# One pass over the tokens, weights packed for single reads, x transposed by layout, and pooling by doubling sums on VectorE, in a hybrid decoder layer on eight cores

## The chip, the cores and the metric

The kernel runs on all 8 cores of one Trainium2 chip. Each core works on its own half of one of four sequences (2048 tokens), so no core waits for another core's data. The metric is the device time of the slowest core, in microseconds (us).

Some executions show a slower state: the cores of one die, or of both, have a lower granted TensorE clock in the records, and the run is some per cent longer. Cores 0 to 3 are die 0, cores 4 to 7 are die 1.

## The reference, cut to what matters

This is an outline and not the code itself.

```python
D_MODEL = 2048; BATCH = 4; SEQ = 4096            # 3 branches of width 1024 each
POOL_WINDOWS = (2, 4, 8, 16)

h = rmsnorm(x, norm_pre)
xa, ga, u, vb, gb, q, gc = split_cols(h @ w_in)  # w_in: 2048 x 7168
ya = pool_mixer(xa, w_pool, scale) * silu(ga)    # A: trailing means minus token, then 256x256 map per group
yb = spatial_gating(u, vb, ...) * silu(gb)       # B: 128x128 causal mixing within chunks of 128 tokens
yc = memory_cross_attention(q, k_m, v_m) * silu(gc)   # C: 4 heads, 256 memory tokens
y = concat([rmsnorm(ya, g_a), rmsnorm(yb, g_b), rmsnorm(yc, g_c)])
out = x + rmsnorm(y @ w_out, norm_post)          # w_out: 3072 x 2048
```

The pool mixer averages, for each of four channel groups, the last 2, 4, 8 or 16 tokens, subtracts the token itself, and applies a 256 x 256 map. Each branch needs a sum of squares over its 1024 channels for every token; both kernels compute it with matmuls against a column of ones, one result column for each tile of 128 tokens.

## The kernel before

The kernel goes over its 2048 tokens in two passes of 1024, and reads the input and output weights once in each pass. It loads x with tokens on the partitions, normalises it, and transposes it on TensorE. In each pass the order is: v and spatial gating (B), pooling (A), attention (C), projection out.

```python
D = 2048; TC = 2048; TP = 1024; NPASS = TC // TP
...
def w_view(src_d, c0):       # 256 columns of the weight: runs of 1 KB in memory
    return src_d[:, c0:c0 + 256].rearrange("(k p) c -> p k c", p=128)
...
def finish_y(p, br, chunk_in_br, tb, pre_fn, pre_reads):
    flush_ss(keep=1)         # the sum of squares of an earlier chunk; the last one stays back
    ...
    P.op("dve", lambda e: pre_fn(e, tmp), ...)
    P.op("act", ... yT3[:, c, ...] = tmp * gain ...)
    P.op("act", ... sq = Square(tmp) ...)
    def ss_group():
        ...                  # 4 matmuls, lhsT=sq (128 tokens each), rhs=ones column
    guard["pending_ss"].append(ss_group)
...
for p in range(NPASS):
    ...
    norm_transpose_many(items, norm_pre_d, after_b=after_b)   # x in, 16 transposes a tile on TensorE
    ...
    xcp_tok = dma_sp(out_d[p * TP:(p + 1) * TP, :], x_d[p * TP:(p + 1) * TP, :], sem="d_xcp")
    for g in range(4):       # pooling: band matrices on TensorE
        ...
        fns += [mm(o, xa_tm[:, tt + 1, cols], mcur[:, g, :], True, False),
                mm(o, xa_tm[:, tt, cols], mprev[:, g, :], False, True)]
```

The copy of x into the output (the residual is added to it at the end by an accumulating DMA) is issued once a pass, at the start of pooling. And a chunk's sum-of-squares matmuls are held back (`keep=1`) until the chunk after it has been emitted, so that TensorE has other work while ScalarE squares.

## Time and profile before

| | before |
|---|---|
| time, median of 3 runs | 1513.77 us (1500.56 to 1519.29) |
| TensorE busy, profiled core | 1281 of 1513 us |
| first steady TensorE work | at 106 us |
| dense stretch: 712 matmuls of 512 columns | 153.7 us, 215.9 ns each |
| read from memory, profiled core | 231 MB |

The first lines are from the page of the kernel before: busy time and share of the span by engine; then the span in 40 slices, in tenths, for TensorE, for its granted clock and for the DMA engines; then the DMA queue of the weights (packets, MB, share of the engines' time) and the memory traffic.

```profile
PE 1281.3 (85%) x7936; PEld 732.4 (48%) x7936; DVE 437.6 (29%) x704; ACT 513.9 (34%) x936; POOL 109.0 (7%) x109
...
PE   0267869999996999999970579899999999999991
...
PEclk9988979999998999999995789999999999999996
DMA  9974999885669954454599959995955364414549
...
q0 software_dynamic: 160400, 109.58, 60.0%
...
HBM read 230.93 MB, written 33.55 MB: 175 GB/s over the span
```

TensorE is the limit: it is busy 85% of the time, and most slices read 9. What is lost lies at the start, in the middle where the second pass begins, and at the end. The windows view of the same kernel gives the busy time of five engines in each stretch (with instruction counts), then the granted clock, the DMA share and GB/s:

```profile
106.00:218.00 112.00, 84.32 (x632) 60.84 (x632) 46.70 (x78) 48.59 (x72) 6.85 (x6) 0.87 0.78 135
240.00:400.00 160.00, 160.00 (x1125) 98.42 (x1123) 34.66 (x56) 42.09 (x78) 12.55 (x11) 1.00 0.74 76
...
782.00:857.00 75.00, 18.38 (x117) 12.71 (x116) 18.64 (x21) 11.48 (x19) 6.66 (x7) 0.60 1.06 194
857.00:968.00 111.00, 90.80 (x697) 66.32 (x695) 49.53 (x84) 54.56 (x82) 6.86 (x6) 0.91 0.87 151
```

The dense stretch (240 to 400 us) has nothing to give: TensorE is busy for all of it at clock 1.00. The change of pass (782 to 857 us) has 18 us of matmuls in 75 us with the DMA engines full. The TensorE timeline of that place (start, duration, work, and in brackets the idle time before it with its releaser) shows what it waited for:

```profile
825.51 1.86 PE L312 MATMUL ps<-ident,yT 128*128 128x128 bf16 x16 [39.34 <-DVE stat L279]
...
835.04 7.09 PE L309 MATMUL ps<-wpool,hT 128*128 128x256 bf16 x48 [5.14 <-DMA out<-stg]
853.60 3.57 PE L309 MATMUL ps<-wpool,hT 128*128 128x256 bf16 x16 [11.47 <-DMA wpool<-w_in]
```

Normalisation, the stores of the first pass and the weights are all late there, one after the other.

### The profile page before, as it was taken

How to read it: one execution, taken by the hardware profiler on the slowest of the kernel's cores; microseconds unless marked ns; L12 is line 12 of the kernel's file. 1: busy time of each engine (PE TensorE's matmuls, PEld its weight loads, DVE VectorE, ACT ScalarE, POOL GpSimd, SP SyncE). 2: the span in 40 equal slices, each digit the busy share in tenths (PEclk: the TensorE clock that was granted, in tenths of full speed). 3: DMA queues.
4: the chain of work that ended last, by engine and by line, in shares of the span. 5: the costliest groups of instructions: out<-in, count | busy, mean ns of one | idle time of the engine just before them, and what ended most of it. 6: DMA issues, size and time to landing. Idle time of an engine off the chain costs nothing.

```text
span 1513.0 us, 20596 instructions; the slowest of 8 cores (1488.0 to 1513.0 us)
## 1 busy us (share of the span) xinstructions
PE 1281.3 (85%) x7936; PEld 732.4 (48%) x7936; DVE 437.6 (29%) x704; ACT 513.9 (34%) x936; POOL 109.0 (7%) x109
## 2 busy tenths in 40 slices
PE   0267869999996999999970579899999999999991
PEld 0156624467774445444430466445776444444440
DVE  0335412311110222322271244222111222232253
ACT  0345412223230465422221354222322466532220
POOL 2000100000011000000011001001000000000000
PEclk9988979999998999999995789999999999999996
DMA  9974999885669954454599959995955364414549
GB/s 150 202 182 120 164 112 102 87 85 57 68 71 154 130 80 56 56 78 67 65 155 204 203 134 167 114 110 56 107 62 65 48 81 67 77 15 70 84 77 146
DMA packets 171135, 156.23 MB, mean 103 GB/s; under 512 B 6560, under 2 KB 165024, under 8 KB 165792
## 3 DMA queue, kind: packets, MB, share of 16 engines
q0 software_dynamic: 160400, 109.58, 60.0%
q1 hardware_dynamic: 10640, 45.34, 13.2%
q8 instruction: 65, 1.06, 0.3%
q14 instruction: 30, 0.25, 0.1%
HBM read 230.93 MB, written 33.55 MB: 175 GB/s over the span
## 4 chain that ended last, share of the span: by engine, by line
PE 74%; DMA 14%; DVE 3%; issue 2%; ACT 2%; SPq 2%; another core or an unknown queue 1%; POOL 0%; DVEq 0%; ACTq 0%; POOLq 0%
PE ps L309 73%; DMA wpool<-w_in 7%; DMA out<-stg 3%; DMA yT<-mem_norm 1%; DMA yT<-norm_pre 1%; SPq L358 1%; DMA yT<-sgu_ln_g 1%; PE ps L312 1%; ACT stg L651 1%; DVE stg L887 1%; SPq L321 1%; ACT junk L633 1%; ACT junk L630 1%; DVE yT L368 0%
## 5 line engine op out<-in xcount | busy, mean ns | idle before, releaser
L309 PE MATMUL ps<-hT,wpool 128*128 128x512 bf16 x2560 | 572.5, 382 | 21.9 <-DMA wpool<-w_in 21.9
L309 PEld LDWEIGHTS ps<-hT,wpool 128*128 128x128 bf16 x2560 | 248.6, 98 | 311.2 <-issue 31.6
L309 PE MATMUL ps<-wpool,yT 128*128 128x512 bf16 (+1 forms) x1600 | 339.8, 375 | 0.0
L309 PE MATMUL ps<-wpool,hT 128*128 128x256 bf16 x2048 | 246.0, 285 | 39.2 <-ACT stg L651 21.7
L309 PEld LDWEIGHTS ps<-wpool,yT 128*128 128x128 bf16 x1600 | 155.9, 98 | 180.9
L309 PEld LDWEIGHTS ps<-wpool,hT 128*128 128x128 bf16 x2048 | 208.2, 102 | 72.9 <-issue 40.9
L522 ACT ACTIVATE yT<-stg,gbr 128x512 bf16<-128x512 f32 x96 | 68.8, 716 | 222.1 <-DVE stg L697 150.7
L312 PE MATMUL ps<-ident,yT 128*128 128x128 bf16 x304 | 27.7, 264 | 123.3 <-DVE stat L279 101.2
L324 POOL DMA_DIRECT2D wpool<-w_in x56 | 64.2, 1158 | 808.8 <-PE ps L309 426.4
L550 ACT ACTIVATE stg<-ps 128x512 f32<-128x512 f32 x96 | 55.5, 596 | 113.7 <-PE ps L309 113.4
L312 PEld LDWEIGHTS ps<-ident,yT 128*128 128x128 bf16 x304 | 24.6, 120 | 126.3 <-issue 126.0
L915 DVE SCALAR_TENSOR_TENSOR hT<-ps,stat,hT 128x512 f32<-128x512 f32 x64 | 48.1, 751 | 91.3 <-PE ps L309 80.7
L683 DVE TENSOR_TENSOR stg<-ps,stg 128x512 f32<-128x512 f32 x32 | 22.1, 692 | 174.5 <-PE ps L309 170.1
L564 DVE CAST stg<-ps 128x512 bf16<-128x512 f32 x32 | 22.1, 692 | 131.8 <-PE ps L309 130.9
L526 ACT ACTIVATE stg<-stg 128x512 bf16<-128x512 f32 x96 | 58.8, 613 | 0.0
L918 ACT ACTIVATE junk<-hT 128x512 bf16<-128x512 f32 x32 | 20.2, 630 | 106.9 <-DVE hT L915 84.2
L763 DVE SCALAR_TENSOR_TENSOR stg<-ps,pscale,stg 128x512 f32<-128x512 f32 x32 | 22.6, 747 | 106.0 <-PE ps L532 106.0
L368 DVE SCALAR_TENSOR_TENSOR yT<-yT,stat 128x2048 bf16<-128x2048 f32 x19 | 44.7, 2352 | 28.8 <-DMA yT<-norm_pre 24.3
L365 ACT ACTIVATE yT<-yT 128x2048 bf16<-128x2048 f32 x19 | 36.1, 1902 | 39.5 <-DMA yT<-x 39.5
L324 POOL DMA_DIRECT2D wpool<-w_out x24 | 21.0, 874 | 345.5 <-PE ps L309 161.8
L564 DVE CAST vnr<-ps 128x256 bf16<-128x256 f32 x32 | 13.6, 425 | 100.4 <-PE ps L309 89.7
L279 DVE RECIPROCAL stat<-stat 128x1 f32<-128x1 f32 (+1 forms) x53 | 8.9, 167 | 112.9 <-ACT stat L277 112.9
(98 smaller groups left out, 886.1 us busy)
## 6 DMA issues: line engine op xcount, KB each, us to landing
wpool<-w_in POOLq DMA_DIRECT2D x56, 1024.0 KB, 23.0
wpool<-w_out POOLq DMA_DIRECT2D x24, 1024.0 KB, 11.5
yT<-x SPq DMA_DIRECT2D x16, 1024.0 KB, 11.3
wpool<-w_kv POOLq DMA_DIRECT2D x8, 1024.0 KB, 13.0
out<-hT POOLq DMA_DIRECT2D x8, 1024.0 KB, 15.3
out<-vnr POOLq DMA_DIRECT2D x4, 1024.0 KB, 22.2
out<-stg POOLq DMA_DIRECT2D x4, 1024.0 KB, 26.9
yT<-mem SPq DMA_DIRECT2D x2, 1024.0 KB, 23.4
```

Source lines behind the costliest of these rows:

```text
L309: return lambda e: e.matmul(out, lhsT=lhsT, rhs=rhs, start=start, stop=stop)
L312: return lambda e: e.transpose(out, in_, ident[:])
L324: return P.op("pool", lambda e: e.dma_start(out=out, in_=in_), reads, writes, dma_sem=sem)
L365: P.op("act", lambda e: e.activation(out=xs, in_=xt, func=AF.Square, accum_out=sc(col_ss)), reads=[xb], writes=[xsb, stb], waits=guard.get ...
L368: P.op("dve", lambda e: e.scalar_tensor_tensor(out=xs, in0=xt, scalar=sc(col_rs), in1=gb_v, op0=ALU.mult, op1=ALU.mult), reads=[xb, gbc, s ...
L522: P.op("act", lambda e: e.activation(out=yT3[:, c, tb * 512:(tb + 1) * 512], in_=tmp, func=AF.Copy, scale=gbr[:, c:c + 1]), reads=[tmp_b[i ...
L526: P.op("act", lambda e: e.activation(out=sq, in_=tmp, func=AF.Square), reads=[tmp_b[i]], writes=[sq_b[i]])
L550: P.op("act", lambda e: e.activation(out=stg_sil[i], in_=psb(b), func=AF.Silu), reads=[bank[b]], writes=[sil_b[i]])
L564: P.op("dve", lambda e: e.tensor_copy(out=out, in_=in_), reads=reads, writes=writes, waits=waits)
L683: P.op("dve", lambda e, si=si, bu=bu: e.tensor_tensor(out=stg_sil[si], in0=psb(bu), in1=stg_sil[si], op=ALU.mult), reads=[bank[bu], sil_b[ ...
L763: return e.scalar_tensor_tensor(out=tmp, in0=psb(by), scalar=pscale[:, ch:ch + 1], in1=stg_sil[si], op0=ALU.mult, op1=ALU.mult)
L915: P.op("dve", lambda e, b=bks[br], orow=orow, c=rc + br * 8 + tt: e.scalar_tensor_tensor(out=orow, in0=psb(b), scalar=sc(c), in1=orow, op0 ...
```

## The change

The intent is to remove everything that happens twice and everything that only moves data on TensorE: one pass over 2048 tokens, so each input weight is read once; weights repacked so that a partition reads 8 KB in a row; x handed over already transposed; the pooling means by doubling sums on VectorE (a window of 16 takes four shifted additions) in place of band matmuls; the output projection in two groups of 7 and 9 token tiles. Branch order becomes A, C, B. Cut to its core, with cuts marked:

```diff
-TP = 1024
-NPASS = TC // TP
...
-    def w_view(src_d, c0):
-        return src_d[:, c0:c0 + 256].rearrange("(k p) c -> p k c", p=128)
+    w_d = din("wst", [NCH, 128, 2048])            # packed
+    def load_group(key, waits=()):
+        ...
+            dma_pool(dst, w_d[c], writes=[M_ring(sl)], sem=f"d_w{sl}", waits=waits)
...
-        norm_transpose_many(items, norm_pre_d, after_b=after_b)
+    def norm_x(tb):                                # x transposed by layout
+        ... Square on ScalarE; 16 matmuls against a 128x128 block of ones
+        rstd_bc(b, 512)                            # Sqrt, then reciprocal of 128x512
+        ... 16 multiplies of 128x512 on VectorE
...
+    late = []
+    def flush(n=0):
+        while len(late) > n:
+            late.pop(0)()
+    def pair_ss(br, tb, first, last):
+        P.op("pool", lambda e: e.tensor_tensor(out=sqp[:], in0=sq[0][:], in1=sq[1][:], op=ALU.add), ...)
+        def f():
+            ... P.group("pe", fns, reads=[M_sqp, "ones"], writes=[bk(0)])   # 4 one-column matmuls
+        late.append(f)
...
-                            fns += [mm(o, xa_tm[:, tt + 1, cols], mcur[:, g, :], True, False),
-                                    mm(o, xa_tm[:, tt, cols], mprev[:, g, :], False, True)]
+    def a_block(g, tb, split=False):
+        for cc in range(2):
+            ... proj(r0 + cc, tb, b, split and cc == 0)
+            a_chain(g, cc, tb, b)                  # copy, 1 to 4 additions, combine (VectorE)
+            if cc == 0:
+                flush()
+        ... 2 more projections with silu
+        def pool_part():
+            ... 4 matmuls, scale on VectorE, finish_y (ScalarE), twice
+            pair_ss(0, tb, g == 0, g == 3)         # appends to late again
+        late.append(pool_part)
...
-        xcp_tok = dma_sp(out_d[p * TP:(p + 1) * TP, :], x_d[p * TP:(p + 1) * TP, :], sem="d_xcp")
+    for j in range(4):                             # emitted in the gating branch
+        ...
+        xcp.append(dma_sp(out_d[j * 512:(j + 1) * 512, :], x_d[j * 512:(j + 1) * 512, :], sem=f"d_xc{j}"))
...
+    for half in range(2):                          # projection out, 7 and then 9 tiles
```

## The prediction

> **What bounds the kernel now.** TensorE. The page's busy table gives PE 1281 of 1513 us; the chain that ended last is 73% matmul. Dense stretches cannot shrink: in the windows 240–400, 640–760 and 1320–1480 us PE is 100% busy at granted clock 1.00, and 712 matmuls of 512 columns take 153.7 us (215.9 ns each). The loss, by windows and chain: PE works steadily only from 106 us; the first v stage runs from 106 to 218 us for about 57 us of matmuls, the second (after an empty stretch, 782–857) to 968; weight waits end both (44 and 36 us) and another comes before the memory projection (31 us); 33 us of tail. Matmuls counted from the program at dense rates (216, 109 and 60 ns for 512, 256 and up to 128 columns) make about 1249 us, so about 264 us are idle or slow clock.
>
> **What changes.** One pass removes the boundary (about 130 us lost at 780–968), the second read of the input weights (184 MB to 126 MB of source), and the 1 KB runs of the weight DMAs. Transposed x removes 304+ transposes and their evictions, but adds 64 ones-matmuls and 16 VectorE multiplies of 512 per block. Pool matmuls leave PE for two to five VectorE operations per half-group. Matmul work falls only to about 1227 us.
>
> **New cost, from the built order on PE.** In the pooling branch each block's deferred part is emitted after the next block's first projection, and its own sum-of-squares matmuls immediately follow. These wait for: ScalarE copy (0.6), 1–4 adds of 512 (0.7 each and about 0.1 between, as dependent VectorE operations show), combine (0.75), two scale operations, copy and square twice (in the trace 3.2 us from the first scale to the last square), then a GpSimd add. The Trainium skill, GPSIMD Engine Reference, section 3.1, has 4497 ns for a 2048-element add; estimate 1.2 us for 512; no add on GpSimd is in this trace. PE covers 0.9 us of it, so stalls of 6.4–8.8 us, and near 19 us where a block's normalisation stands ahead on VectorE (twice; 13 for memory). Sixteen flushes: about 153 us. The Trainium skill, TensorE: Matmul & The Clock Gate, Part 1, says about 3.4 us idle drops the clock; the trace agrees (64 short matmuls take 9.3 us after a pause, 7.15 dense; clock 0.83–0.87 in the v stages). About 2 us per stall: 30 us.
>
> **Sum (estimate).** Steady PE start 54 us (4 MB of x, normalisation, 2 more MB at about 200 GB/s, the rate of busy slices) + 1227 + 153 + 30 + 20 (branch joins, first output weights, half change) + 31 tail = 1515 us. All of it is critical, as PE is: pooling stalls about return the gains.
>
> **What would show it.** First steady PE work 50–65 us; no gap near half time; in the pooling stage (to about 500 us) PE 60–65% busy with a regular 6–9 us gap per block before the one-column matmuls, released by POOL, clock under 0.95; attention, gating and output above 95% busy at 1.00; DMA share lower.
>
> **What would make it wrong.** A GpSimd add under 0.5 us or over 3; the clock not falling in stalls (−25 us); x arriving late (+20); dense matmuls throttled below 1.00 because PE is busier (+5% or more); output weights, read twice, falling behind 12 us per 2 MB.
>
> Predicted 1515 us, 1462–1568 eight times in ten; faster by over 2%: 0.28, within 2%: 0.48, slower: 0.24.

## The result and the profile after

| | before | after |
|---|---|---|
| time, median of fast runs | 1513.12 us (4 runs) | 1589.63 us (4 runs, 1587.03 to 1593.79) |
| ratio after / before | | 1.052, 95% interval 1.0448 to 1.0591 |
| read from memory | 231 MB | 165 MB |
| TensorE busy | 1281 us | 1298 us |
| first steady TensorE work | 106 us | 51 us |

Ratios here are the mean time of one kernel's fast runs over that of the other's fast runs of the same rounds, so they are not quite the ratio of the medians quoted. The changed kernel is correct, and slower. The prediction was wrong: it had said 1515 us, with 1568 at the top of its range, and had given "slower" 0.24.

The same lines of the page of the kernel after, with the two groups that matter (line, engine, operation, shapes, count, then busy time, mean ns, idle time before them and what ended it):

```profile
PE 1297.9 (82%) x6242; PEld 588.7 (37%) x6242; DVE 525.0 (33%) x868; ACT 434.5 (27%) x781; POOL 126.4 (8%) x165
...
PE   2755457777675896699998999999998999799990
...
PEclk9887779798887787799999999999998999899995
DMA  9910109333300599703303006033125559973279
...
q0 software_dynamic: 21136, 80.22, 33.1%
...
HBM read 164.93 MB, written 33.55 MB: 125 GB/s over the span
...
L510 PE MATMUL ps<-arena 128*128 128x1 bf16 x192 | 11.7, 165 | 158.9 <-POOL arena L503 158.9
...
L503 POOL TENSOR_TENSOR arena<-arena 128x512 bf16<-128x512 bf16 x48 | 55.1, 1148 | 891.9 <-ACT arena L499 878.4
```

The DMA engines are much freer, the gap in the middle is gone, and TensorE starts in half the time. But the first third of the span now reads 4 to 7 in the busy slices and 7 to 9 in the clock slices: that is the pooling branch, which runs to 537 us. The waits view (line waited at, what ended the wait, total us, times, longest) names three waits of TensorE:

```profile
PE ps L510 <- POOL arena L503: 158.9, 19, 19.3
PE ps L364 <- ACT arena L430: 43.7, 13, 15.6
PE ps L364 <- DMA arena<-wst: 42.9, 3, 28.2
```

The first is the one that matters. The second is mostly the start, while x arrives. One case of the first, from the timeline of all engines, with L531 a doubling addition, L537 the combination, L577 the scale by gate, L496 and L499 the scaled copy and the square on ScalarE, L503 the addition on GpSimd and L510 the one-column matmuls:

```profile
74.31 0.69 DVE L531 TENSOR_TENSOR arena<-arena 128x512 f32<-128x512 f32 x1 [0.83 <-ACT arena L525]
75.11 0.69 DVE L537 SCALAR_TENSOR_TENSOR arena<-arena 128x512 bf16<-128x512 f32 x1
...
76.02 1.41 DVE L577 SCALAR_TENSOR_TENSOR arena<-ps,arena 128x512 f32<-128x512 f32 x2
...
78.63 0.61 ACT L499 ACTIVATE arena<-arena 128x512 bf16<-128x512 f32 x1
79.39 1.14 POOL L503 TENSOR_TENSOR arena<-arena 128x512 bf16<-128x512 bf16 x1 [58.73 <-ACT arena L499]
...
80.68 0.24 PE L510 MATMUL ps<-arena 128*128 128x1 bf16 x4 [6.31 <-POOL arena L503]
```

This is one chain of dependent work, with TensorE standing idle for 6.31 us of it. The reason is in the source: `flush` runs the deferred `pool_part`, which appends the sum of squares to the same list, and the `while` loop runs that at once. Deferral works for the matmuls of the pooling map and not for the sum of squares behind them.

The second cost is the clock, and it shows best in windows of 2 us around one such stall, which here lasts from 274.3 to 281.18 us (columns as above; the third number from the end is the clock):

```profile
276.00:278.00 2.00, 0.00 (x0) 0.00 (x0) 1.81 (x3) 0.75 (x2) 0.00 (x0) 1.00 0.93 174
278.00:280.00 2.00, 0.00 (x0) 0.00 (x0) 0.00 (x0) 1.62 (x3) 0.11 (x1) 0.63 0.38 76
...
283.00:285.00 2.00, 2.00 (x6) 0.71 (x5) 0.00 (x0) 0.00 (x0) 0.00 (x0) 0.50 0.62 92
...
287.00:289.00 2.00, 2.00 (x11) 0.94 (x10) 1.15 (x2) 0.58 (x1) 0.53 (x1) 1.00 0.02 4
```

About 4 us into the pause the clock falls to 0.50. It stays there until about 4 us after work has resumed: TensorE does 6 matmuls in 2 us where it later does 11. "Busy" does not show this. The mean clock of the whole window 260 to 537 us is 0.83, but that is not a level at which TensorE ever runs for long: it is a mixture of 1.00 and 0.50, and of one more level that comes next. The Trainium skill, TensorE: Matmul & The Clock Gate, Part 1, has this gate: half clock after an idle window of about 3.4 us, full clock after as long a stretch of work. This trace agrees: over the 16 stalls of pooling on core 6, the clock fell 2.1 to 5.2 us after the pause began and came back 3.1 to 6.1 us after work had resumed.

The third cost comes in attention. These are the TensorE timeline there; then the issues of SyncE's queue; then the DMA views, by queue for 560 to 620 us, in which both queues had work (packets, MB and share of the engines' time), and by issue for 530 to 660 us (KB each and median us from issue to landing):

```profile
620.41 0.70 PE L701 MATMUL ps<-arena 128*128 128x128 bf16 x8
649.29 10.99 PE L364 MATMUL ps<-arena 128*128 128x512 bf16 x39 [28.18 <-DMA arena<-wst]
```

```profile
533.68 2.54 SPq L368 DMA_DIRECT2D out<-x  x4
```

```profile
q1 hardware_dynamic: 169, 8.52, 81.9%
q0 software_dynamic: 176, 0.66, 13.7%
...
arena<-wst POOLq DMA_DIRECT2D x8, 512.0 KB, 56.3
...
out<-x SPq DMA_DIRECT2D x4, 74.1
```

The four copies of x into the output (4 MB each) stand in the gating branch in the source, in a loop that runs from about 970 us. But nothing that they wait for ties them to it, so SyncE issues them as soon as it comes to them, at 533.68 us, the moment when attention loads its second group of weights. That group landed around 649 us, and TensorE waited 28 us for it. From 560 to 620 us the two queues sent nearly equal numbers of packets (169 and 176), but those of the copies' queue are larger, 50 KB against 4 KB on average (MB over packets), so it had 82% of the engines' time. The Trainium skill, DMA: Bandwidth & Descriptors, section on queues, rings and completion order, says that an engine alternates between its queues packet by packet; the two counts agree with it, if the profile's packets are those that the page means.

There is a fourth, smaller thing. On cores 2, 3, 6 and 7 the clock read 0.81 whenever it was not 0.50, from about 500 to 659 us, through dense work; on cores 0, 1, 4 and 5 attention ran at 1.00. Core 6 ended at 1589.1 us and core 0 at 1577.5.

### The profile page after: what moved, and what is told of

Its sections match the earlier page's. It is cut to its first block, busy times and chain, and to the rows that moved or that the text cites. A ratio compares the mean times of both kernels' runs of the same rounds, so it can differ in the third digit from the quotient of the medians.

```text
span 1589.1 us, 17429 instructions; the slowest of 8 cores (1577.5 to 1589.1 us)
## 1 busy us (share of the span) xinstructions
PE 1297.9 (82%) x6242; PEld 588.7 (37%) x6242; DVE 525.0 (33%) x868; ACT 434.5 (27%) x781; POOL 126.4 (8%) x165
## 4 chain that ended last, share of the span: by engine, by line
PE 76%; DVE 8%; ACT 4%; DMA 4%; issue 3%; another core or an unknown queue 2%; POOL 1%; DVEq 0%; ACTq 0%; POOLq 0%; SPq 0%
PE ps L364 75%; DVE arena L439 2%; DMA arena<-wst 2%; DVE arena L531 2%; DMA arena<-xT 2%; POOL arena L503 1%; ACT arena L499 1%; ACT arena L430 1%; DVE arena L577 1%; DVE arena L420 1%; ACT arena L496 1%; DVE arena L949 1%; DVE arena L537 1%; PE ps L510 1%
## 5 line engine op out<-in xcount | busy, mean ns | idle before, releaser
L364 PE MATMUL ps<-arena 128*128 128x512 bf16 (+3 forms) x5922 | 1289.6, 380 | 94.9 <-ACT arena L430 43.7
L364 PEld LDWEIGHTS ps<-arena 128*128 128x128 bf16 x5922 | 574.7, 101 | 785.2 <-issue 236.5
L496 ACT ACTIVATE arena<-arena 128x512 bf16<-128x512 f32 x96 | 68.8, 716 | 428.8 <-DVE arena L839 173.1
L931 DVE SCALAR_TENSOR_TENSOR arena<-ps,arena 128x512 f32<-128x512 f32 x128 | 95.9, 750 | 204.0 <-PE ps L364 184.9
L510 PE MATMUL ps<-arena 128*128 128x1 bf16 x192 | 11.7, 165 | 158.9 <-POOL arena L503 158.9
L531 DVE TENSOR_TENSOR arena<-arena 128x512 f32<-128x512 f32 (+5 forms) x80 | 55.7, 697 | 224.3 <-ACT arena L525 219.3
L503 POOL TENSOR_TENSOR arena<-arena 128x512 bf16<-128x512 bf16 x48 | 55.1, 1148 | 891.9 <-ACT arena L499 878.4
L935 ACT ACTIVATE ps<-arena 128x512 f32<-128x512 f32 x64 | 38.5, 601 | 227.5 <-DVE arena L931 191.9
L371 POOL DMA_DIRECT2D arena<-wst x96 | 56.5, 601 | 453.0 <-PE ps L364 434.6
L833 DVE SCALAR_TENSOR_TENSOR arena<-ps,arena 128x512 f32<-128x512 f32 x32 | 24.0, 751 | 154.8 <-PE ps L364 83.3
L510 PEld LDWEIGHTS ps<-arena 128*128 128x128 bf16 x192 | 9.6, 100 | 173.3 <-issue 172.8
L517 ACT ACTIVATE arena<-ps 128x512 f32<-128x512 f32 x64 | 37.1, 596 | 82.5 <-PE ps L364 81.9
L499 ACT ACTIVATE arena<-arena 128x512 bf16<-128x512 f32 x96 | 58.8, 613 | 0.0
L928 ACT ACTIVATE arena<-ps,arena 128x512 f32<-128x512 f32 x64 | 43.3, 683 | 24.6 <-PE ps L364 11.7
L439 DVE SCALAR_TENSOR_TENSOR arena<-arena 128x512 bf16<-128x512 f32 x64 | 42.8, 745 | 0.4
## 6 DMA issues: line engine op xcount, KB each, us to landing
arena<-wst POOLq DMA_DIRECT2D x72, 512.0 KB, 13.5
out<-arena POOLq DMA_DIRECT2D x16, 1024.0 KB, 14.9
```

The costliest lines, as they stand in the source:

```text
L364: return lambda e: e.matmul(out, lhsT=lhsT, rhs=rhs, start=start, stop=stop)
L371: return P.op("pool", lambda e: e.dma_start(out=out, in_=in_), reads, writes, waits, dma_sem=sem)
L439: P.op("dve", lambda e, i=i, k=k: e.scalar_tensor_tensor(out=hT[:, k, tb * 512:(tb + 1) * 512], in0=xp[i % 6][:, k % 4, :], scalar=cp[:, C ...
L496: P.op("act", lambda e: e.activation(out=yT[:, c, tb * 512:(tb + 1) * 512], in_=tmp[ti][:], func=AF.Copy, scale=cp[:, CP_GBR + c:CP_GBR + ...
L499: P.op("act", lambda e: e.activation(out=sq[si][:], in_=tmp[ti][:], func=AF.Square), reads=[M_tmp[ti]], writes=[M_sq[si]])
L503: P.op("pool", lambda e: e.tensor_tensor(out=sqp[:], in0=sq[0][:], in1=sq[1][:], op=ALU.add), reads=[M_sq[0], M_sq[1]], writes=[M_sqp])
```

## The experiments

The theory: the time went into (1) stalls of TensorE at the sum of squares, (2) a lower clock, and (3) the weights that arrive behind the copies. Rivals: that the lower clock does not belong to the stalls but to the first part of the kernel or to all cores working at once, and that the wait in attention is not due to the copies. Experiments e1, e2, e3 and e4 ran where the kernel before had many slow runs (its two fast ones took 1511.54 and 1512.35 us); e3 again, e5 and e6 where it took 1510.15 us (median of 11).

### e1: hold the sum of squares back by one more block

```diff
-    def flush(n=0):
-        while len(late) > n:
+    def flush():
+        for _ in range(len(late)):
             late.pop(0)()
...
     def branch_rstd():
-        flush()
+        while late:
+            flush()
```

> Edit: each flush emits only what was waiting when it began, so a pooling block's sum-of-squares matmuls come one block (about 15 us of TensorE work) later than the pool matmuls they depend on. Theory P (placement): the 159 us that PE waits for the GpSimd add in front of these matmuls fall below 30 us. Rival V (the VectorE work itself, norms and doubling sums, cannot keep up): the wait only moves to pool matmuls or to PSUM banks, and the time stays above 1540 us. On the clock, theory B (the stop-and-go of the pooling stage trips the lower clock): granted clock in the dense pooling stretches and in attention goes from about 0.81 to 1.00, time 1390 to 1440 us. Rival E (the clock is low in the first 600 us for another cause): clock stays 0.81 to about 620 us and the time is 1450 to 1490 us.

Correct; one fast run, 1423.77 us, and three slow ones. The waits view of core 0, which had an undisturbed die:

```profile
PE ps L364 <- DMA arena<-wst: 57.0, 3, 43.5
...
PE ps L510 <- POOL arena L503: 12.0, 4, 5.3
```

On core 0 the wait for GpSimd fell from 159.2 to 12.0 us. The span of that core fell from 1577.5 to 1416.9 us, by more than the wait, because the clock came back with it: adding up windows of 1 us (busy time times one minus the clock), the time that TensorE lost to a lower clock fell from 53 to 19 us. Part was given back: the wait for weights grew from 48.5 to 57.0, since attention now starts earlier and runs into the same copies.

### e2: tie the copies of x to the gating branch

```diff
             pair_ss(1, tb, j == 0, j == 3)
+            if tb == 0:
+                xcp.append(dma_sp(out_d[j * 512:(j + 1) * 512, :], x_d[j * 512:(j + 1) * 512, :],
+                                  sem=f"d_xc{j}", waits=[("e_pe", P.count["e_pe"])]))
...
-    xcp.append(dma_sp(out_d[...], x_d[...], sem=f"d_xc{j}"))
```

> Edit: the four copies of x into the output wait for TensorE to reach the gating stage, instead of all starting together where attention starts. Theory D (the 28 us wait for weights at 621 us is this collision): the wait goes, the copies land in the gating stage. On the clock: if the lower clock is released by time or by the end of the bursts, the gain is about 28 us (1561 us). If it was released by the 28 us pause itself, the attention stage goes on at 0.81 after 650 us and the gain is eaten: 1580 us or slower, in the worst case 1650.

Correct; the three fast runs took 1561.40, 1561.97 and 1583.40 us (two more were slow), ratio to before 1.04 (1.0087 to 1.0713), too wide an interval to call it slower by 2%. The wait of TensorE at GpSimd is unchanged, 158.9 us. The weights wait of the slowest core fell from 42.9 to 14.6 us, and its longest from 28.2 to 7.3:

```profile
PE ps L364 <- DMA arena<-wst: 14.6, 2, 7.3
```

So the copies were the cause. The gain in time, 28 us (medians of fast runs, 1561.97 against 1589.63), is smaller than what core 0 gained (1577.5 to 1536.9, 41 us). Windows of core 0 and of core 4, the slowest, show why:

```profile
537.00:600.00 63.00, 61.45 (x320) 29.49 (x326) 25.24 (x50) 30.44 (x60) 5.55 (x7) 1.00 0.19 35
```

```profile
540.00:657.00 117.00, 116.06 (x513) 51.84 (x512) 40.83 (x84) 47.33 (x92) 7.84 (x9) 0.81 0.23 35
657.00:720.00 63.00, 62.38 (x337) 29.83 (x335) 24.27 (x49) 29.72 (x59) 6.69 (x8) 0.99 0.21 34
```

Cores 4 and 5 held the clock 0.81 from about 497 to 659 us, through dense work, and then had full clock without any pause. In the kernel after, the cores with the lower clock were partly forgiven it: they arrived later at a wait that ended at a time set by the DMA (28.2 us on core 6, 35.4 on core 0). With that wait gone they pay in full.

### e3: both together

The edits of e1 and e2.

> Both edits. Theories P, B and D together: no wait over 8 us in pooling after the normalisations, clock near 1.00, 1360 to 1410 us, faster than both kernels. If the gains overlap (the pause hides other waits), no better than the deferral alone.

Correct; fast runs 1375.41 and 1395.96 us, ratio 0.9165 with a wide interval (0.8872 to 0.9457), four slow runs.

> The same kernel as in the earlier run of both edits, repeated for a ratio from more fast runs: most runs there were in the slow state. Expected: fast runs at 1370 to 1380 us, ratio to before 0.90 to 0.92.

Median 1375.55 us of five fast runs (a sixth was slow), ratio to before 0.9135 (0.9099 to 0.9171). This version beats both kernels. The windows of core 0 in this repeat, in pooling and in attention:

```profile
200.00:350.00 150.00, 149.20 (x831) 75.39 (x844) 71.05 (x112) 37.73 (x69) 17.75 (x24) 1.00 0.54 89
...
460.00:520.00 60.00, 59.44 (x312) 28.34 (x317) 25.12 (x55) 32.05 (x63) 6.69 (x8) 1.00 0.22 36
```

Pooling now has TensorE busy for 149 of 150 us at clock 1.00, with the additions on VectorE and GpSimd as before. So the place of the work was not the fault; the point where its result was asked for was. From the kernel after to e3, core 0 went from 1577.5 to 1366.9 us, by 211: the wait at GpSimd fell by 147 us (159.2 to 12.2), the weights wait by 36 (48.5 to 12.8), the time lost to the clock by 39 (53 to 14), and other waits grew by about 12. On the same core the first edit alone gave 161 us and the second alone 41, which is 202 of the 211; the other 9 us are about what the first alone had given back in the wait for weights.

### e4: move the flush in front of the additions of the block

A second way to shorten the stall, by a changed order on VectorE alone: the deferred scale operations go ahead of the new block's doubling additions.

```diff
             proj(r0 + cc, tb, b, split and cc == 0)
-            a_chain(g, cc, tb, b)
             if cc == 0:
                 flush()
+            a_chain(g, cc, tb, b)
```

> Edit: in the kernel after, the deferred part is emitted ahead of the next block's doubling sums instead of behind them, sum-of-squares placement unchanged. Theory P as costed: each stall is a sum of terms and loses the ScalarE copy, the sums and the combine, 2.4 to 4.8 us per block, while scale, copy, square, GpSimd add (about 5 us) stay: waits of 159 us fall to about 95 to 110 us, time 1525 to 1545 us. If the doubling sums were not part of the stall, no change.

One fast run, 1537.31 us. The wait at GpSimd fell from 158.9 to 110.5 us, still 19 times:

```profile
PE ps L510 <- POOL arena L503: 110.5, 19, 16.7
```

So 48 us of the stalls were the additions standing ahead on VectorE. Of the rest, three stalls (16.3, 16.7 and 13.5 us) still have a normalisation ahead of them on VectorE, and the others, 4.3 to 4.5 us in pooling, are the chain from the scale to GpSimd. The clock gave nothing back: 76 us of the pooling stage's work still ran at 0.50 on core 2, against 77 on core 6 of the kernel after, with as many stalls, though shorter ones. Time and wait moved together: 52 us of time for 48 of wait. That this run also had a spell of the clock 0.81 on cores 2 and 3 (433 to 576 us), as the kernel after had, leaves a few us of it open.

### e5: put the stall back, in attention

The test for the clock. To e3, one line: after each attention block the sum of squares is asked for at once.

```diff
         pair_ss(2, tb, hh == 0, hh == 3)
+        flush()
```

> Both edits kept, but now the attention stage (another stage, with other VectorE and DMA work) gets the placement that pooling had: its sum-of-squares matmuls right behind the matmuls they depend on. By the chain (two multiplies, copy and square twice, GpSimd add) each of the 16 blocks stalls 4 to 5 us, as the one such place between attention and gating did in the kernel after (4.5 us): 65 to 80 us in all. Theory B (stop-and-go work itself brings the lower clock): on an undisturbed die the granted clock of the attention stage falls from 1.00 to 0.80 to 0.88 and its dense stretches slow by 15 to 20%, a further 25 to 45 us; fast time 1470 to 1500 us. Rival E (the low clock belonged to the pooling stage or to the first 600 us): clock stays at or above 0.95 apart from the pauses, time 1440 to 1455 us.

1483.14 us (two fast runs), ratio to before 0.9835 (0.9788 to 0.9881), 108 us more than e3. All 8 cores lay between 1474.8 and 1480.8 us. Pooling kept its clock of 1.00. Attention on core 0, around one of the new stalls of 4.55 us (416.4 to 420.92 us):

```profile
412.00:417.00 5.00, 4.31 (x20) 1.76 (x18) 2.39 (x5) 0.01 (x1) 0.00 (x0) 1.00 0.00 0
...
423.00:425.00 2.00, 2.00 (x7) 0.62 (x5) 0.96 (x3) 1.59 (x2) 0.00 (x0) 0.50 0.00 0
...
427.00:434.00 7.00, 6.95 (x33) 3.19 (x33) 0.86 (x2) 2.50 (x4) 0.00 (x0) 1.00 0.00 0
```

The wait at GpSimd grew from 12.2 to 80.2 us on core 0, by 68:

```profile
PE ps L510 <- POOL arena L503: 80.2, 19, 5.3
```

From 360 to 820 us, where attention lies, TensorE did 87 us of its work at clock 0.50, against 5 in e3, which is 41 us more lost. The two make 109 of the 110 us by which this core's span grew. The rival that the low clock belongs to the first 600 us or to pooling falls: the same pooling runs at 1.00, and attention, which ran at 1.00 in e3, loses its clock when pauses of 4.5 us are put in. These pauses cost, beyond themselves, more than half as much again in clock (41 us beside 68).

### e6: interleave the blocks with the normalisation

With the stalls gone, the largest wait of e3 is for the squares of x at the start (ScalarE, 51.9 us on core 0). This run emits a pooling block between the normalisations, in the hope of filling it.

```diff
     norm_x(0)
     norm_halo()
-    norm_x(1)
     a_block(0, 0, True)
+    norm_x(1)
+    a_block(1, 0)
     a_block(0, 1, True)
     norm_x(2)
...
```

> Both edits, and the blocks of the first two pooling groups reordered so that a normalisation always has a whole block of matmuls in front of it (first block ahead of the second normalisation; the buffer of the pooled differences rotated so that neighbours do not share it). In the run of both edits TensorE still waited 52 us for the squares and about 12 us for VectorE in the first 200 us. If those waits are only order: 20 to 35 us less, fast runs 1340 to 1355 us. If x arrives too slowly (about 17 MB of x and weights by 100 us), less than 10 us.

A miss: 1389.08 us (median of three fast runs; a fourth was slow), ratio 0.9213 (0.9178 to 0.9248), 14 us slower than e3. The waits of core 0:

```profile
PE ps L364 <- ACT arena L430: 28.4, 14, 11.6
PE ps L364 <- DVE arena L454: 19.7, 1, 19.7
PE ps L510 <- POOL arena L503: 16.2, 5, 5.0
```

The wait aimed at fell by 23.5 us, but a new one of 19.7 took its place: the first block needs the normalised 16 tokens ahead of the half, and those now stand directly in front of it. The later normalisations now stand behind pooling work in the emitted order, and the wait for the memory's squares (L464) grew from 3.4 to 11.8 us. The wait moved, and did not go. What an order that wins here would look like is open.

## Why the prediction was wrong

Two terms of its sum failed: the lower clock (30 us predicted, 72 measured) and the other waits (20 predicted, 58 measured). The sum can be measured term by term. The terms for core 6, the slowest of the profiled run, and for core 0, which had no spell of 0.81, in us. Start is the time to steady matmuls; matmuls are TensorE's busy time after it, less the clock term; the clock term sums busy time times one minus the granted clock over windows of 1 us; other waits are what is left idle before the last matmul.

| term | predicted | core 6 | core 0 |
|---|---|---|---|
| steady start | 54 | 51 | 49 |
| matmuls at full clock | 1227 | 1212 | 1216 |
| pooling stalls | 153 | 159 | 159 |
| lower clock | 30 | 72 | 53 |
| other waits | 20 | 58 | 65 |
| tail | 31 | 37 | 36 |
| sum | 1515 | 1589 | 1578 |

- "Sixteen flushes: about 153 us" was right: 152 us in 16 waits in pooling (158.9 us in 19 waits in all). That it came so close is partly luck, since single stalls lay off (14.9 us where 13 was said; the last block's 4.4). Its chain was right too. The addition on GpSimd was estimated at 1.2 us from the Trainium skill, GPSIMD Engine Reference, section 3.1, and took 1.148. The stalls of "6.4–8.8 us, and near 19 us where a block's normalisation stands ahead" were there: most lay between 6.3 and 9.4 us (6.31, 6.90 and 8.57 are examples), two at 19.2 and 19.3. e1 and e3 show that this one loop was the main loss.
- "Steady PE start 54 us" and the absent gap at half time were right. So was the pooling stage: TensorE was 65% busy from 100 to 500 us, at a mean clock of 0.82. The matmuls came out 11 to 15 us lower, because those of the start were counted in both terms.
- "About 2 us per stall: 30 us" is a term that was mis-sized, though not in what it describes. In pooling, TensorE did 77 us of work at clock 0.50 on core 6, so lost 39 us, 2.4 per stall. e5 shows the mechanism by itself. The term lacked two things. Outside the pooling stalls, about 14 us more are lost at 0.50, at the start, after the waits for weights and at the joins of branches. And core 6 lost about 20 us to the spell at 0.81 (104 us of work, times 0.19), which nothing in the profile of before's slowest core had shown, though other cores of that run had one (see below). The prediction's own list of dangers had the clock only in the other direction ("the clock not falling in stalls") or as a general throttle.
- "20 (branch joins, first output weights, half change)" is the step that failed in kind: it left out the copies of x. Other waits took 58 us, and half of it, 28.2 us, was the wait for attention weights behind the copies of x. The prediction had looked at the traffic as a total ("DMA share lower", which was right) and not at when SyncE would issue the copies. They stand late in the source, but SyncE ran its list as far as its waits allowed, and these had none: the copies were issued at 534 us and not from about 970. e2 shows the effect.
- "Attention, gating and output above 95% busy at 1.00" failed for the same two reasons until 649 us (74% busy at mean clock 0.73 from 537 to 649 us) and held after it (97% at 0.98).
- "Pooling stalls about return the gains" was right in kind and too small by 74 us: 42 from the clock, 38 from other waits, 6 each from stalls and tail, less 18 from the start and the matmuls. On core 0, without the spell, it would still have been too small by 63.

What stays open: why a pair of cores had the clock 0.81 at that time. It is not the changed kernel's own. All of die 1 in the profiled fast run of before had it, core 4 from 99 to 260 us, die 1 of e3's slow run from 161 to 322 us, and cores 4 and 5 of e1 at the same time. These spells lasted about 160 us (that of e4 144) and ended in the middle of dense work. What one costs depends on where it falls: in before it fell largely in the stage that waits for weights, and though cores 4 to 7 lost 47 to 56 us to the clock in the whole run, against 28 to 32 on cores 0 to 3, their spans were no longer (1499 to 1507 us against 1488 to 1513). In e3 it fits what made that run a slow one: 154 us of work at 0.81 lose 29 us, and the span of core 6 was 26 us longer than that of core 0. No experiment here started or stopped it.

## What to carry to other kernels

When work is deferred to hide a chain of small operations, follow what the deferred work itself defers: a queue that is drained "until empty" runs the second half of the chain at once, and in these runs nearly every pause of TensorE over 4 us was paid again as half clock for the first 3 to 6 us of the work after it. A large transfer that waits for nothing can be issued long before its place in the source suggests (here at 534 us and not from about 970), so tie it to the stage that has the bandwidth to spare. And read the clock in windows as short as the pauses: a mean of 0.83 can be full clock and half clock in turn, a single slower level, or both, and here only the first went away with the stalls.

## What the Trainium skill lacked or had wrong

- TensorE: Matmul & The Clock Gate, Part 1, on the clock gate: it agrees with these runs. Its one worked price, about 0.8 us per pause (an estimate from its 26.7 us for 32 pauses), is that of a kernel with about 2 us of matmuls between pauses. Here longer work follows each pause and the price is higher: with 16 pauses of 9.5 us on average in pooling, 77 us of work ran at 0.50, so a pause cost about 2.4 us beyond itself; the 15 added pauses of about 4.5 us in attention (e5) cost no less, about 2.7 us each (41 us).
- The same part, on the peak-current limiter, has a whole die at 13/16 (0.8125) once three of its cores run dense matmuls, held while the load lasts. The level fits (0.81), the rest does not fit these runs: all eight cores ran dense matmuls at 1.00 for most of e3, and the level came for about 160 us (499 to 659, 161 to 322, 99 to 260 us), in several runs on only two cores of a die, and ended while the dense work went on.
- DMA: Bandwidth & Descriptors, on queues, rings and completion order, has the alternation by packet but not what it does to a small transfer beside a large copy: with 169 packets against 176 (560 to 620 us), the queue of the copies from memory to memory took 81.9% of the engines' time, and weight loads of 512 KB took 56.3 us to land (530 to 660 us; 13.5 us over the whole kernel).
- VectorE: DVE Perf Modes says that reciprocal iterates, but gives no duration. In the kernel after, a reciprocal of 128 x 512 in f32 took 3.35 us, against 0.745 us for the multiply of that size beside it; it stood in both stalls near 19 us.
- GPSIMD Engine Reference, section 3.1, has one measured addition, of 2048 elements in f32 (4497 ns). An addition of 512 in bf16 took 1148 ns here, close to a quarter of that.
